# The last outputs of a two-layer decoder in single file, and weight splits behind the additions at the turn of layers

## The chip, the cores and the metric

The kernel runs on one core of one Trainium2 chip. The metric is the time of one execution on the device in microseconds (us), lower is better. TensorE (PE) multiplies into PSUM banks of 512 float32 columns; VectorE (DVE), ScalarE (ACT) and GpSimd (POOL) do the rest; SyncE (SP), ScalarE and GpSimd issue the transfers.

## What is computed

A decoder trunk of two layers on 512 tokens of width 1024, in float32, followed by a norm:

```python
def hybrid_layer(x, ...):
    z = rmsnorm(x, g_mix) @ w_in                 # q, k, v, retention q, k, v, gates
    ya = sliding_window_sink_attention(...) @ w_a
    yb = (group_norm(chunkwise_retention(...)) * silu(rg)) @ w_b
    x = x + (sigmoid(ga) * ya + sigmoid(gb) * yb) @ w_out
    h2 = rmsnorm(x, g_mlp)
    return x + jnp.square(jax.nn.relu(h2 @ w_up)) @ w_down
def reference(x, ...):
    for l in range(2):
        x = hybrid_layer(x, ...)
    return rmsnorm(x, g_final)
```

## The kernel before

**Products in three parts.** Every float32 operand is kept as a sum of two parts, hi (rounded to the matmul's own type) and lo (the rest). A product is three matmuls, hi by hi, hi by lo and lo by hi (`products`, L355 to L357). Weights come in units of 128 x 1024 elements: a DMA on SP's queue into one of five raw buffers, a ScalarE copy into hi (L308) and a VectorE subtraction into lo (L309), four buffers each. `unit` hands out the next unit and splits up to three ahead; `state["hold"]` limits how far ahead, for a while.

**Order.** The program is traced in a written order and then a scheduler with a model of times places each engine's instructions; each engine runs its own queue in the order that results. `with tc.issue_after(ins):` adds an edge that holds an instruction behind `ins` in the queue of the engine that runs `ins`, and only there; it is no wait on a semaphore.

**MLP.** The up and down projections work on blocks of 512 of the 4096 hidden units, the up projection by `pair` in halves of the tokens, the down projection by `down`, which goes through seven sums in PSUM (`multiply(a, b11)` to `multiply(b, u_forms[3])`). Results of a block are added in DRAM into `y` (tokens on partitions) by GpSimd's DMAs. The last block has another receiver, `Ending`.

**The turn of layers** (last block of layer 0). `Ending.put` adds the half i = 0 of the output columns (in `late`) on VectorE (L1352); for i = 1, `join` scales on ScalarE (L1347) and a DMA with addition (L1348) brings it to a tile `y`. `last_but_one` transposes the half i = 0 on TensorE (`turn`, L1389), adds it to x (L1395) and makes the next layer's operands xh (L378) and xl (L379) of it. The other half is turned in `carry`, within layer 1's first group, `group(..., low_last=...)`, whose first two weight units are gone through by `by_halves` (L368): all products with xh first, those with xl last. In between stand the splits of layer 1's first weights.

**The end** (last block of layer 1, `down_plain`). There are eight outputs of 128 tokens x 512 columns, each a sum over four weight units `w_end`, twelve matmuls. Three of them, `early`, go through the four units as these come; five are traced one after the other, the last in two halves of 256 columns (SOON, LATE). For each, `Ending.put` adds on VectorE (L1352), takes the squares' sum on ScalarE (L1367), and for the second half of a block's columns the root (L1375), the reciprocal (L1376) and the scaling of both halves (L1377 on VectorE, L1381 on ScalarE), and writes them out by SP (L1379) and ScalarE (L1382). For the first half it multiplies by the gain (L1369) and prepares a scalar (L1370).

Of the kernel before, what the change touches and what calls it, by code (L numbers as in the profile page):

```python
# [13 lines left out]
ALU = mybir.AluOpType  # L14
# [5 lines left out]
D = 1024  # L20
# [10 lines left out]
EPS = 1e-6  # L31
# [13 lines left out]
N_BLOCK = 8  # L45
# [69 lines left out]
def decoder(ctx, tc, xT, x_first, w_in, w_a, w_b, w_out, w_up, w_pair, w_down, w_end, tables, decay, band, g_last, out):  # L115
    nc = tc.nc
# [232 lines left out]
    def products(ps, pairs, start, stop, resume=False):  # L349


        n = len(pairs)
        for i, ((ah, al), (bh, bl)) in enumerate(pairs):
            more = {"skip_group_check": True} if resume else {}
            nc.tensor.matmul(ps, ah, bh, start=start and i == 0, stop=False, **more)  # L355
            nc.tensor.matmul(ps, ah, bl, start=False, stop=False, **more)  # L356
            nc.tensor.matmul(ps, al, bh, start=False, stop=stop and i == n - 1, **more)  # L357

    def by_halves(banks, weights, moving, ks, cols, meanwhile):

        hi, lo = weights
        for w, low in ((hi, 0), (lo, 0), (hi, 1)):
            if meanwhile and w is lo:
                meanwhile()
            for j, k in enumerate(ks):
                for c, ps in enumerate(banks):
                    first, final = k == 0 and w is hi and not low, k == KD - 1 and low
                    latest[0] = nc.tensor.matmul(ps, w[:, cols(j, c)], moving[k][low], start=first, stop=bool(final)).ins  # L368

    latest = [None]  # L370

    def split(hi, lo, src, scale=None):

# [41 lines left out]
    def group(name, layer, moving, evacuates, meanwhile=None, low_last=None):  # L415


        banks = [bank(ps_mm, "mm") for _ in range(4)]
        for u in range(4):
            if low_last:  # L420
                state["hold"] = state["next"] + 2 if u < 2 else None
            hi, lo = unit(name, layer)
            if low_last:
                by_halves(
                    banks,
                    (hi, lo),
                    moving,
                    (2 * u, 2 * u + 1),
                    lambda j, c: slice(j * T + c * P, j * T + (c + 1) * P),
                    low_last.get(u),  # L430
                )
            for j in range(0 if low_last else 2):
                k = 2 * u + j
                for c, ps in enumerate(banks):
                    cols = slice(j * T + c * P, j * T + (c + 1) * P)
                    products(ps, [((hi[:, cols], lo[:, cols]), moving[k])], k == 0, k == KD - 1)
            if meanwhile and u in meanwhile:
                meanwhile[u]()
        for ps, evacuate in zip(banks, evacuates):
            evacuate(ps)  # L440
# [17 lines left out]
    H = T // 2  # L458
# [116 lines left out]
    def layer_body(layer):  # L575
# [634 lines left out]
        def down_plain(into):  # L1210
            sums.free()

            def inner(k, m):
                if k < 2:
                    parts = [t[:, 2 * k + m // 2, (m % 2) * P : (m % 2 + 1) * P] for t in u_forms.tiles[0][0]]
                else:
                    parts = [u_two[:, r, m * P : (m + 1) * P] for r in (k - 2, k)]
                return tuple(parts)

            def add(ps, m, half, k, at=slice(0, T)):  # L1220
                cols = slice(half * T + at.start, half * T + at.stop)
                hi, lo = units[k]
                products(ps[:, : at.stop - at.start], [(inner(k, m), (hi[:, cols], lo[:, cols]))], k == 0, k == 3)

            units = []
            places = [(m, half) for m in range(NB) for half in range(2)]
            early = [(*place, bank(pool, "mm")) for place, pool in zip(places, (ps_mm, ps_aux, ps_mm))]
            for k in range(4):
                units.append(unit("w_end", layer))
                for m, half, ps in early:  # L1230
                    add(ps, m, half, k)
            for m, half, ps in early:
                into.put(half, m // 2, m % 2, ps, 1)
            for m, half in places[len(early) :]:
                final = (m, half) == places[-1]
                for at in (SOON, LATE) if final else (slice(0, T),):
                    ps = bank(ps_mm, "mm")
                    for k in range(4):
                        add(ps, m, half, k, at)
                    into.put(half, m // 2, m % 2, ps[:, : at.stop - at.start], 1, at)  # L1240

        def down(e, into):
            def multiply(ps, moving, start=True):
                hi, lo = unit("block", layer)
                for m in range(2):
                    at = slice(m * P, (m + 1) * P)
                    pairs = []
                    for k, (uh, ul) in enumerate(moving):
                        cols = slice(k * T, (k + 1) * T)
                        pairs.append(((uh[:, at], ul[:, at]), (hi[:, cols], lo[:, cols])))  # L1250
                    products(ps[m], pairs, start, True, not start)

            b11 = [(first_hi[:, k, :], first_lo[:, k, :]) for k in range(2)]
            b21, b22 = (
                [(u_two[:, k, at], u_two[:, 2 + k, at]) for k in range(2)] for at in (slice(0, H), slice(H, T))
            )
            if e == N_BLOCK - 1:
                sums.free()
            a, c = ([bank(ps_mm, "mm") for _ in range(2)] for _ in range(2))
            b = [bank(ps_aux, "b") for _ in range(2)]  # L1260
            multiply(a, b11)
            for m in range(2):
                nc.scalar.activation(b[m], a[m], AF.Copy)
            multiply(c, u_forms[0])
            for m in range(2):
                into.early(1, 1, m, c[m], -1)
            multiply(b, u_forms[1], False)
            for m in range(2):
                into.early(0, 1, m, b[m], 1)
            multiply(a, b21, False)  # L1270
            for m in range(2):
                into.put(0, 0, m, a[m], 1)
            multiply(c, b22, False)
            for m in range(2):
                into.put(0, 1, m, c[m], 1)
            if e == N_BLOCK - 1:
                state["hold"] = state["next"] + 3
            multiply(b, u_forms[2], False)
            for m in range(2):
                into.put(1, 1, m, b[m], -1)  # L1280
            into.last_but_one()
            multiply(b, u_forms[3], False)
            for m in range(2):
                into.put(1, 0, m, b[m], -1)
            into.end()
# [36 lines left out]
        class Ending:  # L1322


            def __init__(self):
                self.y, self.queued = {}, []
                for i, j in ((1, 1), (0, 1), (0, 0), (1, 0)):
                    if last:
                        two = x[:, 4 * j + 2 * i : 4 * j + 2 * i + 2, :]
                    elif i == 0:  # L1330
                        two = late_box[0][:, 2 * j : 2 * j + 2, :]
                    else:
                        two = big("y")
                    nc.gpsimd.dma_start(two, y[:, 2 * j : 2 * j + 2, i * T : (i + 1) * T])
                    for m in range(2):
                        self.y[i, j, m] = two[:, m, :]
# [17 lines left out]
            def put(self, i, j, m, ps, sign, at=slice(0, T)):  # L1354
                block = 2 * j + m
                scale = (factor if sign > 0 else negative)[:, block : block + 1]
                if i and not last:
                    self.join(i, j, m, ps, scale)
                    return
                with ExitStack() as behind:  # L1360
                    for ins in self.queued if i else ():
                        behind.enter_context(tc.issue_after(ins))
                    self.add(i, j, m, ps, scale, at)
                if last:
                    v = self.y[i, j, m]
# [1 line left out]
                    nc.scalar.activation(temp("junk")[:, at], v[:, at], AF.Square, accum_out=both if i else first)  # L1367
                    if not i:
                        nc.vector.tensor_tensor(v, v, last_gain[:, i, :], ALU.mult)  # L1369
                        self.queued.append(nc.vector.tensor_scalar(first, first, 1.0 / D, EPS, ALU.mult, ALU.add).ins)  # L1370
                        return
                    if at.stop < T:
                        nc.vector.scalar_tensor_tensor(first, both, 1.0 / D, first, ALU.mult, ALU.add)
                        return
                    nc.scalar.activation(total, both, AF.Sqrt, bias=first, scale=1.0 / D)  # L1375
                    nc.vector.reciprocal(total, total)  # L1376
                    final = nc.vector.scalar_tensor_tensor(v, v, total, last_gain[:, 1, :], ALU.mult, ALU.mult)  # L1377
                    self.queued = [final.ins]
                    nc.sync.dma_start(out[:, block, T:], v)  # L1379
                    v = self.y[0, j, m]  # L1380
                    nc.scalar.activation(v, v, AF.Copy, scale=total)  # L1381
# [2 lines left out]
            def turn(self, i, j, half, pool):  # L1384
# [7 lines left out]
                            ident,  # L1392
                        )
                xa = x[:, 4 * i + 2 * half : 4 * i + 2 * half + 2, j * H : (j + 1) * H]
                nc.vector.tensor_tensor(xa, xa, ps.rearrange("p (a t) -> p a t", t=H), ALU.add)  # L1395

            def last_but_one(self):
                if not last:
                    for half in range(2):
                        for j in range(2):  # L1400
                            self.turn(0, j, half, ps_mm)
                        for k in (2 * half, 2 * half + 1):
                            self.behind = scaled_input(k, g_mix + 2)

            def end(self):
                if not last:
# [219 lines left out]
```

## Time and profile before

| what | value |
|---|---|
| median of three runs | 1486.21 us (1484.3 to 1486.42) |
| the profiled execution's own time | 1484.08 us |
| its span, first to last instruction | 1482.3 us |
| TensorE busy | 1464.7 us |
| VectorE, ScalarE, GpSimd busy | 1079.1, 915.3, 192.6 us |
| mean granted TensorE clock | 0.997 |

A row of a timeline is: start, duration, engine, line, operation, output <- inputs, partitions x elements, count, and in brackets the engine's idle time before it with what ended it. Rows that overlap on one engine are pipelined. A row of the waits is: who waited for whom, microseconds in total, times, longest.

### The profile page before, as it was taken

The numbers are of one execution on the slowest core, as the hardware profiler recorded it, in microseconds if no ns is written. First come the engines' busy times: TensorE is split into PE (matmuls) and PEld (weight loads), VectorE is DVE, ScalarE is ACT, GpSimd is POOL, SyncE is SP. The second block draws the span as 40 slices with busy tenths as digits, with TensorE's granted clock in tenths as the row PEclk, the third lists the DMA queues.
The fourth block names the chain that finished last, engine by engine and source line by source line (L and its number), as shares of the span: only waits on it lengthen the run. The fifth ranks groups of instructions, "written<-read, shape, count | busy, mean of one in ns | idle before, by whom it ended". The sixth has DMA issues, their size and how long they took to land.

```text
span 1482.3 us, 21312 instructions
## 1 busy us (share of the span) xinstructions
PE 1464.7 (99%) x7799; PEld 1265.3 (85%) x7799; DVE 1079.1 (73%) x1639; ACT 915.3 (62%) x1501; POOL 192.6 (13%) x282
## 2 busy tenths in 40 slices
PE   9999999999999999999999999999999999999996
PEld 7888888888889999998888888888888899999995
DVE  6877668664677888888877785687447688887874
ACT  7647345532467777777765573556325777777773
POOL 0101111101001111112101012110000111111120
PEclk9999999999999999999999999999999999999998
DMA  7663996668316777776947449976443377777772
GB/s 260 186 177 98 311 265 176 178 193 215 113 51 198 192 194 190 196 183 186 304 143 211 142 131 302 250 213 161 142 128 106 105 193 188 198 192 190 194 209 90
DMA packets 92984, 272.61 MB, mean 184 GB/s; under 512 B 10832, under 2 KB 10960, under 8 KB 89040
## 3 DMA queue, kind: packets, MB, share of 16 engines
q1 hardware_dynamic: 60816, 169.27, 33.6%
q0 software_dynamic: 31344, 100.68, 31.0%
q8 instruction: 61, 1.00, 0.3%
q10 hardware_dynamic: 720, 1.31, 0.2%
q14 instruction: 43, 0.35, 0.1%
HBM read 231.37 MB, written 99.09 MB: 223 GB/s over the span
## 4 chain that ended last, share of the span: by engine, by line
PE 98%; DVE 1%; ACT 1%; DMA 0%; issue 0%; ACTq 0%
PE mm L355 25%; PE mm L357 25%; PE mm L356 25%; PE b L355 3%; PE b L356 3%; PE b L357 3%; PE rv L355 2%; PE rv L357 2%; PE rv L356 2%; PE mm L368 2%; PE score L734 1%; PE pT L699 1%; PE r L356 1%; PE r L357 1%; PE r L355 1%; PE pv L720 0%
## 5 line engine op out<-in xcount | busy, mean ns | idle before, releaser
L308 ACT ACTIVATE hi<-raw 128x1024 fp32r<-128x1024 f32 (+1 forms) x363 | 369.8, 1019 | 331.6 <-PE mm L356 224.1
L309 DVE TENSOR_TENSOR lo<-raw,hi 128x1024 fp32r<-128x1024 f32 (+1 forms) x364 | 423.7, 1170 | 168.7 <-ACT hi L308 167.5
L355 PE MATMUL mm<-xh,hi 128*128 128x512 f32 (+1 forms) x976 | 344.5, 355 | 1.1 <-ACT xh L378 0.7
L356 PE MATMUL mm<-xl,hi 128*128 128x512 f32 (+1 forms) x976 | 343.1, 354 | 0.0
L357 PE MATMUL mm<-xh,lo 128*128 128x512 f32 (+1 forms) x976 | 341.3, 355 | 0.0
L355 PE MATMUL mm<-r,hi 128*128 128x256 f32 (+1 forms) x736 | 238.6, 324 | 0.5 <-ACT mm L1181 0.5
L357 PE MATMUL mm<-r,lo 128*128 128x256 f32 (+1 forms) x736 | 238.9, 325 | 0.0
L356 PE MATMUL mm<-r,hi 128*128 128x256 f32 (+1 forms) x736 | 238.8, 324 | 0.0
L355 PEld LDWEIGHTS mm<-xh,hi 128*128 128x128 f32 x976 | 184.7, 189 | 25.8 <-ACT xh L378 1.3
L356 PEld LDWEIGHTS mm<-xl,hi 128*128 128x128 f32 x976 | 184.7, 189 | 24.2
L357 PEld LDWEIGHTS mm<-xh,lo 128*128 128x128 f32 x976 | 183.7, 189 | 24.3
L355 PEld LDWEIGHTS mm<-r,hi 128*128 128x128 f32 x736 | 139.8, 190 | 13.8 <-ACT mm L1181 0.7
L356 PEld LDWEIGHTS mm<-r,hi 128*128 128x128 f32 x736 | 139.8, 190 | 13.1
L357 PEld LDWEIGHTS mm<-r,lo 128*128 128x128 f32 x736 | 139.8, 190 | 11.3
L1320 POOL DMA_DIRECT2D y<-eu x56 | 62.2, 1353 | 370.1 <-DVE eu L1305 370.1
L356 PE MATMUL mm<-lo,r 128*128 128x512 f32 (+1 forms) x276 | 104.4, 387 | 0.0
L357 PE MATMUL mm<-hi,r 128*128 128x512 f32 (+1 forms) x276 | 101.5, 386 | 0.0
L355 PE MATMUL mm<-hi,r 128*128 128x512 f32 (+1 forms) x276 | 98.2, 389 | 0.3 <-ACT r L375 0.2
L355 PE MATMUL b<-hi,r 128*128 128x512 f32 x180 | 70.4, 391 | 0.0
L1320 POOL DMA_DIRECT2D y<-y x56 | 55.8, 1010 | 111.6 <-ACT y L1315 105.7
L356 PE MATMUL b<-lo,r 128*128 128x512 f32 x180 | 70.2, 390 | 0.0
L357 PE MATMUL b<-hi,r 128*128 128x512 f32 x180 | 67.8, 389 | 0.0
(271 smaller groups left out, 2333.1 us busy)
## 6 DMA issues: line engine op xcount, KB each, us to landing
raw<-w_in_in SPq DMA_DIRECT2D x89, 512.0 KB, 5.5
sums_down<-w_down_in POOLq DMA_DIRECT2D x30, 1024.0 KB, 11.0
sums_up<-w_pair_in POOLq DMA_DIRECT2D x56, 512.0 KB, 10.2
raw<-w_down_in SPq DMA_DIRECT2D x45, 512.0 KB, 7.5
raw<-w_pair_in SPq DMA_DIRECT2D x84, 256.0 KB, 3.7
y<-y POOLq DMA_DIRECT2D x64, 256.0 KB, 8.7
y<-eu POOLq DMA_DIRECT2D x62, 256.0 KB, 8.3
raw<-sums_down SPq DMA_DIRECT2D x30, 512.0 KB, 7.0
```

Source lines behind the costliest of these rows:

```text
L308: nc.scalar.activation(hi[:, at], raw[:, at], AF.Copy)
L309: nc.vector.tensor_tensor(lo[:, at], raw[:, at], f32(hi[:, at]), ALU.subtract)
L355: nc.tensor.matmul(ps, ah, bh, start=start and i == 0, stop=False, **more)
L356: nc.tensor.matmul(ps, ah, bl, start=False, stop=False, **more)
L357: nc.tensor.matmul(ps, al, bh, start=False, stop=stop and i == n - 1, **more)
L368: latest[0] = nc.tensor.matmul(ps, w[:, cols(j, c)], moving[k][low], start=first, stop=bool(final)).ins
L699: nc.tensor.transpose(pt[:, i * P : (i + 1) * P], sm[:, at : at + P], ident)
L734: nc.tensor.matmul(ps[:, g * w : (g + 1) * w], q_s[g][:, c, at], part[:, keys], start=i == 0, stop=i == 1)
L1320: nc.gpsimd.dma_start(y[:, 2 * j + m, i * T : (i + 1) * T], t, **how)
```

## The change

Two places change. **At the end**, `products` now records its last matmul in `latest[0]`, and each of the five outputs of `down_plain` that follow the early ones is traced under `issue_after(latest[0])`: on TensorE it stands whole behind the output before it. In `put`, an addition of the second half is queued behind the last scalar step of a first half only, no longer behind the scaling of the block before.

**At the turn of layers**, the hold on splits is set one product of `down` earlier; the split of layer 1's first unit is done by `first_weights`, on VectorE behind the two additions to x of the first half of the turned columns; the splits of the second and third unit are queued on ScalarE and VectorE behind the xh and xl of the first and of the second half (`behind`).

```diff
@@ products
-            nc.tensor.matmul(ps, al, bh, start=False, stop=stop and i == n - 1, **more)
+            latest[0] = nc.tensor.matmul(ps, al, bh, start=False, stop=stop and i == n - 1, **more).ins
+
+    latest, behind = [None], []
@@ group
         for u in range(4):
-            if low_last:
-                state["hold"] = state["next"] + 2 if u < 2 else None
-            hi, lo = unit(name, layer)
+            with ExitStack() as queue:
+                if low_last:
+                    state["hold"] = state["next"] + 2 if u < 2 else None
+                for ins in behind.pop(0) if behind else ():
+                    queue.enter_context(tc.issue_after(ins))
+                hi, lo = unit(name, layer)
@@ down_plain
                     ps = bank(ps_mm, "mm")
-                    for k in range(4):
-                        add(ps, m, half, k, at)
+                    with tc.issue_after(latest[0]):
+                        for k in range(4):
+                            add(ps, m, half, k, at)
@@ down
+            if e == N_BLOCK - 1:
+                state["hold"] = state["next"] + 3
             multiply(c, b22, False)
             for m in range(2):
                 into.put(0, 1, m, c[m], 1)
-            if e == N_BLOCK - 1:
-                state["hold"] = state["next"] + 3
             multiply(b, u_forms[2], False)
...
             multiply(b, u_forms[3], False)
+            if e == N_BLOCK - 1:
+                into.first_weights()
             for m in range(2):
                 into.put(1, 0, m, b[m], -1)
@@ Ending.put
-                with ExitStack() as behind:
-                    for ins in self.queued if i else ():
-                        behind.enter_context(tc.issue_after(ins))
+                with tc.issue_after(self.queued) if i else ExitStack():
                     self.add(i, j, m, ps, scale, at)
...
-                        self.queued.append(nc.vector.tensor_scalar(first, first, 1.0 / D, EPS, ALU.mult, ALU.add).ins)
+                        self.queued = nc.vector.tensor_scalar(first, first, 1.0 / D, EPS, ALU.mult, ALU.add).ins
...
-                    final = nc.vector.scalar_tensor_tensor(v, v, total, last_gain[:, 1, :], ALU.mult, ALU.mult)
-                    self.queued = [final.ins]
+                    nc.vector.scalar_tensor_tensor(v, v, total, last_gain[:, 1, :], ALU.mult, ALU.mult)
@@ Ending
+            def first_weights(self):
+                with tc.issue_after(self.turned):
+                    split_until(state["next"] + 1)
+
             def last_but_one(self):
                 if not last:
                     for half in range(2):
                         for j in range(2):
-                            self.turn(0, j, half, ps_mm)
+                            turned = self.turn(0, j, half, ps_mm)
                         for k in (2 * half, 2 * half + 1):
                             self.behind = scaled_input(k, g_mix + 2)
+                        if half == 0:
+                            self.turned = turned
+                            behind.append(self.behind)
+                    behind.append(self.behind)
```

`turn` now returns the instruction of its addition.

More of the change, by code (lines that the diff above doesn't have):

```diff
@@ L368, in by_halves @@
                     latest[0] = nc.tensor.matmul(ps, w[:, cols(j, c)], moving[k][low], start=first, stop=bool(final)).ins
-    latest = [None]
     def split(hi, lo, src, scale=None):
@@ L1325, in __init__ @@
             def __init__(self):
-                self.y, self.queued = {}, []
+                self.y, self.queued = {}, None
                 for i, j in ((1, 1), (0, 1), (0, 0), (1, 0)):
@@ L1394, in turn @@
                 xa = x[:, 4 * i + 2 * half : 4 * i + 2 * half + 2, j * H : (j + 1) * H]
-                nc.vector.tensor_tensor(xa, xa, ps.rearrange("p (a t) -> p a t", t=H), ALU.add)
+                return nc.vector.tensor_tensor(xa, xa, ps.rearrange("p (a t) -> p a t", t=H), ALU.add).ins
+            def first_weights(self):
+                with tc.issue_after(self.turned):
+                    split_until(state["next"] + 1)
             def last_but_one(self):
```

## The prediction

> **What bounds the kernel now.** I read the page first, then the waits of TensorE, then busy time by stretch, and last the timeline of the two places that the change touches.
>
> ```profile
> span 1482.3 us, 21312 instructions
> PE 1464.7 (99%) x7799; PEld 1265.3 (85%) x7799; DVE 1079.1 (73%) x1639; ACT 915.3 (62%) x1501; POOL 192.6 (13%) x282
> ```
>
> TensorE is busy for 1464.7 of 1482.3 us, and the change removes no product. It can only win from the 17.6 us in which TensorE is idle. Where those lie, the waits of TensorE and the stretches tell:
>
> ```profile
> PE mm L368 <- ACT xh L378: 1.7, 1, 1.7
> PE warm L335 <- DVE ones L330: 1.1, 1, 1.1
> PE mm L355 <- DVE z L853: 0.5, 1, 0.5
> ```
>
> ```profile
> 54.00:180.00 126.00, 126.00 (x613) 105.63 (x612) 92.28 (x233) 71.49 (x154) 16.43 (x30) 1.00 0.69 199
> 770.00:892.00 122.00, 121.55 (x597) 101.91 (x596) 95.32 (x243) 75.90 (x163) 12.06 (x20) 1.00 0.55 159
> 1469.60:1482.30 12.70, 0.00 (x0) 0.00 (x0) 5.68 (x14) 5.70 (x16) 0.00 (x0) 0.61 0.34 126
> ```
>
> In the second fence the columns are the stretch, its length, and the busy time of TensorE, its weight loads, VectorE, ScalarE and GpSimd. The last row is the one that matters: for 12.7 us after the last product the chip only adds, squares, scales and writes out. The wait of 1.7 us is the turn of layers (L368 is the first product of layer 1). The upper two rows are the attention of layers 0 and 1; there is next to nothing to win there.
>
> **The end: what the change does to it.** In the built program of before, TensorE's queue weaves the outputs of L1236–1239 into each other and into the three early ones; all eight finish late and in a bunch. In the changed program every output of twelve products stands whole behind the one before it. The products are the same.
>
> ```profile
> 1448.00 1.08 PE L355 MATMUL mm<-hi,r 128*128 128x512 f32 x4
> ...
> 1453.51 0.28 PE L356 MATMUL mm<-r,hi 128*128 128x256 f32 x1
> ...
> 1453.75 0.40 PE L355 MATMUL mm<-hi,r 128*128 128x512 f32 x1
> ...
> 1466.47 0.28 PE L355 MATMUL mm<-hi,r 128*128 128x256 f32 x1
> ...
> 1469.22 0.28 PE L357 MATMUL mm<-hi,r 128*128 128x256 f32 x1
> ```
>
> ```profile
> 1453.83 1.06 ACT L308 ACTIVATE hi<-raw 128x1024 fp32r<-128x1024 f32 x1 [3.53 <-PE mm L356]
> ...
> 1455.64 0.42 ACT L375 ACTIVATE r<-z 128x256 fp32r<-128x256 f32 x1
> ...
> 1476.60 0.42 ACT L1367 ACTIVATE junk<-x 128x256 f32<-128x256 f32 x1 [0.23 <-DVE sq L1373]
> ```
>
> ```profile
> 1456.10 0.42 DVE L376 TENSOR_TENSOR r<-z,r 128x256 fp32r<-128x256 f32 x1
> 1461.46 0.75 DVE L1352 SCALAR_TENSOR_TENSOR x<-mm,columns,x 128x512 f32<-128x512 f32 x1 [4.94 <-PE mm L357]
> ...
> 1467.34 0.74 DVE L1377 SCALAR_TENSOR_TENSOR x<-x,sq,late 128x512 f32<-128x512 f32 x1
> ...
> 1471.01 0.75 DVE L1377 SCALAR_TENSOR_TENSOR x<-x,sq,late 128x512 f32<-128x512 f32 x1
> ...
> 1475.35 0.87 DVE L1352 SCALAR_TENSOR_TENSOR x<-mm,columns,x 128x256 f32<-128x256 f32 x2
> 1476.40 0.16 DVE L1373 SCALAR_TENSOR_TENSOR sq<-sq 128x1 f32<-128x1 f32 x1 [0.18 <-ACT junk L1367]
> ```
>
> Between 1453.75 and 1466.47 stand 56 products, so one of 512 columns takes 0.227 us; 23 steps of 256 columns from 1466.47 to 1469.22 give 0.120. The first addition starts only at 1461.46, when TensorE is two thirds through; from there a block of 128 tokens costs VectorE and ScalarE 3.67 us (L1377 at 1467.34 and 1471.01), and the last addition runs at 1475.78, 6.3 us after its products ended at 1469.50.
>
> *The weight wait moves.* Ten products of later outputs (six of one, four of another) stood ahead of the up-projection's last twelve products (the 256-wide ones on `r`). Now they stand behind. Those twelve end 10 x 0.227 = 2.27 us sooner, the last weight split (L308, released by their L356 at 1453.79) starts at 1451.56 instead of 1453.83, and what follows it on both engines shifts by as much: L375 ends at 1453.79, L376 at 1454.25.
>
> *TensorE waits in return.* Nine products of the third weight unit run from 1453.75 - 2.27 = 1451.48 to 1453.52; the next needs L375's result, at 1453.82 with the 0.04 that such a step takes. No other product may pass, so 0.30 us are lost that before were filled with later outputs. Its rows near the end of before start in the order of the built program. The Trainium skill, "TensorE: Matmul & The Clock Gate", Part 2 (What happens when you issue a matmul), says that only weight loads are pulled ahead while matmuls keep program order, which speaks against this queue; by it the end costs those 0.30 us, without it none. The sum has the 0.30.
>
> *The drain.* Products now end at 1469.50 + 0.30 = 1469.80. Outputs finish every 12 x 0.227 = 2.72 us, two of them (5.45 us) to a block, against the 3.67 us that a block costs afterwards, so both engines are through with everything older when the last half arrives (the first three outputs end near 1455.6 now: 1453.82 + 6 x 0.227 + 0.39 of one product). Which scalar step the additions of half 1 are queued behind (`self.queued`) changes with it and costs nothing, as VectorE is waiting for TensorE here; without that cover it would be one step, 0.7 us. Step by step in the new order of VectorE: the seventh output is ready at 1466.95, its addition, the scaling of the block before and the gain product take to about 1469.1, the addition of the first half to 1469.5, then it waits. The last addition runs 1469.82 to 1470.25 (half of 0.87), L1373 behind it at 1470.27. From L1373 to the span's end there were 1482.3 - 1476.40 = 5.90 us, a chain of single steps on one half-width output that no edit touches. End: 1476.17, **6.1 us less**. Bounds: 6.4 without the 0.30; 3.8 if the weight split doesn't move and TensorE waits for L376's operand as late as before (another 2.3).
>
> **The turn of layers.**
>
> ```profile
> 729.95 0.82 PE L1389 MATMUL turn<-ident,late 128*128 128x128 f32 x6
> ...
> 734.48 2.12 PE L368 MATMUL mm<-xh,hi 128*128 128x512 f32 x8 [1.68 <-ACT xh L378]
> ...
> 741.90 1.47 PE L1389 MATMUL turn<-ident,y 128*128 128x128 f32 x12
> ```
>
> ```profile
> 728.96 1.22 DVE L309 TENSOR_TENSOR lo<-raw,hi 128x1024 fp32r<-128x1024 f32 x1
> ...
> 730.76 1.22 DVE L309 TENSOR_TENSOR lo<-raw,hi 128x1024 fp32r<-128x1024 f32 x1
> 731.89 1.91 DVE L1395 TENSOR_TENSOR x<-x,turn 128x512 f32<-128x512 f32 x3
> ```
>
> ```profile
> 732.19 0.69 ACT L1347 ACTIVATE eu<-b,columns 128x512 f32<-128x512 f32 x1 [1.19 <-PE b L357]
> 732.77 1.05 ACT L308 ACTIVATE hi<-raw 128x1024 fp32r<-128x1024 f32 x1
> 733.72 1.32 ACT L378 ACTIVATE xh<-x 128x512 fp32r<-128x512 f32 x2
> 734.95 0.62 ACT L506 ACTIVATE acc<-x 128x512 f32<-128x512 f32 x1
> ```
>
> Before, two splits on VectorE (728.96, 730.76) and one on ScalarE (732.77) stand ahead of the additions to x and the first xh. In the changed program they stand behind. All twelve transposes of `late` now go together at 729.95; from 0.82 for six and 1.47 for twelve each adds 0.11, so the ninth, the last that half 0 of x needs, ends at 731.1. VectorE takes the two additions that are ready at 730.7 and 731.3 (spacing 0.61 by the row of three); the second ends at 731.99. ScalarE starts xh at 732.01 and TensorE can go 0.76 later (733.72 to 734.48 in before): 732.77. TensorE itself is free at 734.48 - 1.68 = 732.80. The wait of 1.68 goes; nothing is left of it.
>
> *What is late next.* The second result of L1347 at this place (732.19) now stands behind two xh, one split and one square: 732.01 + 1.23 (733.72 to 734.95) + 0.95 (732.77 to 733.72) + 0.62 = 734.8. GpSimd adds it to y by DMA, and transposes in layer 1's first group need it.
>
> ```profile
> 733.24 0.85 POOL L1348 DMA_DIRECT2D y<-eu  x1 [0.94 <-ACT eu L1347]
> ```
>
> ```profile
> DMA to landing us min/median/max: 5.2/6.8/8.6
> ```
>
> ```profile
> DMA to landing us min/median/max: 8.6/8.6/8.6
> ```
>
> The first answer is for the six transfers of this line near the turn, the second for this one. Before, it landed at 733.24 + 8.6 = 741.84, and TensorE came for it at 741.90: just in time. Now it is issued 1.05 us after 734.8, at 735.85, and lands between 741.05 and 744.45. TensorE, 1.68 us ahead, does 32 products by 740.22 (7.42 us as before), then six transposes that need only older parts (0.65) and six products (1.39), and asks at 742.26. The stall is 0 to 2.2 us; I take the median row, 742.65, thus 0.4, since the loads that L309 releases (five buffers) start later and leave the transfer more room than before. The Trainium skill, "DMA: Bandwidth & Descriptors", Anatomy of one DMA, gives 2.0 us plus bytes over 436 GB/s, an estimate of 2.6 us for 256 KB: then nothing would stall and the turn would give 1.7; the rows here, 5.2 at the least, decide.
>
> *Other queues.* On SP two spills now go ahead of a weight load that waits for the moved L309; issued near 733.1 it lands 5.5 us later, and its split ran at 747.06, so 8 us cover it:
>
> ```profile
> raw<-w_in_in SPq DMA_DIRECT2D x89, 512.0 KB, 5.5
> ```
>
> ```profile
> 747.06 1.06 ACT L308 ACTIVATE hi<-raw 128x1024 fp32r<-128x1024 f32 x1 [0.80 <-PE mm L368]
> ```
>
> The moved VectorE split of the first unit (to 733.05) is needed by the ninth product, at 734.7. The hold on splits is set one product earlier (ahead of `multiply(c, b22, ...)`), which leaves the splits of the last two down units where they are in both programs and moves only the one above. The turn gives 1.68 - 0.4 = **1.3 us**, from 1.7 down to a loss of 0.5. Behind it the scheduler also orders layer 1's attention anew. Two orders of it stand in the trace, with 0.00 and 0.45 us of idle TensorE in the stretches above; I book 0, bounds -0.45 to +0.5.
>
> **Sum.** 6.1 + 1.3 = 7.4 us. The profiled execution took 1484.08 (span 1482.3 and 1.8 around it); it becomes 1476.7. It lies 2.1 under the median of the runs (1486.21, lowest 1484.3); on the median it is 1478.8. The likeliest case runs from 1475.6 (all upper bounds, 6.4 + 1.7 + 0.45 = 8.5, off the profiled execution) to 1480.5 (5.7 off the median, just short of the first rival).
>
> **Rivals.**
> *Late transfer* (14%): the moved DMA lands after 8.6 us as its like did; the turn loses 0.5, the end gives 6.1: 1480.6 by the median. For it: the DMA was just in time before. Against: fewer loads beside it.
> *Split not released* (9%): the last weight split stays where it was, TensorE stalls 2.3 us more in its fixed order: 6.1 - 2.3 + 1.3 = 5.1, 1481.1. For it: L308 waits for a buffer and for TensorE. Against: its row names TensorE's L356, which moves.
> *Bunching stays* (4%): additions and squares still go in the old pace because their own queues, not the products' order, hold them; 12.7 us of drain remain and only the turn pays: 1484.9, no change that can be measured. Against: the first addition waited 4.94 us for TensorE, by its row.
> *Attention exposed* (5%), the slower one: in the new order each of the 16 score steps of layer 1 lets TensorE wait for ScalarE's exponential.
>
> ```profile
> DVE st L758 <- ACT st L757: 4.4, 8, 1.3
> ```
>
> At the longest 1.3 us each that is 20.8 us: 1478.8 + 20.8 = 1499.6. It turns the sign beyond noise from 0.65 us a step (10.4 us). Against it: 126.00 of 126.00 us busy in layer 0's attention.
>
> **Chances.** The forecast has 68%; faster by over 0.2% (about 3 us, what a measurement here can tell from no change) takes it and the first two rivals, 0.91 together, shaded to 0.88 for what I have not seen; same 0.06, slower 0.06. The range leaves out the last two rivals: 1475.6 to 1482.
>
> **What would show it.** Right: no TensorE wait at L368 or under 0.5 us at the transposes of y; first addition of the end near 1455.6 on before's clock; about 6.4 us between last product and span's end. Wrong: a wait of TensorE for `y`; more than 1 us of wait in the last 20 us; new waits in layer 1's attention.

## The result, and the profile after

The changed kernel takes 1478.39 us (median of 8 runs, 1477.88 to 1483.20), the kernel before 1484.20 (median of 8 runs beside it, 1483.68 to 1486.45). The ratio is 0.9963, with a 95% interval of 0.9951 to 0.9974: 5.5 us faster by the means, 5.8 by the medians. One of the eight runs, at 1483.20, stands alone above the others and has no trace. Predicted were 1478.8 (1475.6 to 1482.0) and, in gain, 7.4 us. The predicted time came so near partly by luck: it was taken off a median of 1486.21, and the median of the longer series is 2.0 lower, while the gain of the medians is 1.6 smaller than the sum. The account below is of the gain.

In the changed kernel's own lines the products of the first group are L370 (L368 before), the transposes L1392 (L1389), the additions to x L1398 (L1395), the copy and the transfer into y L1353 and L1354 (L1347, L1348), the additions at the end L1358 (L1352), the last scaling L1381 (L1377), and the scaling that forms z L856 (L853).

The page and the waits of TensorE (us in all, times, longest):

```profile
span 1478.6 us, 21314 instructions
PE 1467.4 (99%) x7799; PEld 1266.5 (86%) x7799; DVE 1079.6 (73%) x1639; ACT 914.0 (62%) x1501; POOL 195.3 (13%) x282
...
PE mm L355 <- DVE z L856: 1.0, 1, 1.0
PE turn L1392 <- DMA y<-eu: 0.9, 1, 0.9
PE mm L355 <- ACT xh L378: 0.8, 1, 0.8
```

This execution took 1480.34 us, its span is 1478.6. The wait of 1.7 us at the turn is gone. Two others have grown: TensorE waits 0.9 us for the transfer into y, which stood nowhere before, and 1.0 instead of 0.5 for z. And TensorE seems to work more, 1467.4 us against 1464.7. Most of that has nothing to do with the change: 2.0 us of it are the start of this execution. The timeline of the first products, first of before, then of after:

```profile
5.45 1.17 PE L355 MATMUL mm<-xh,hi 128*128 128x512 f32 x4 [0.67 <-ACT xh L378]
6.46 1.08 PE L356 MATMUL mm<-xl,hi 128*128 128x512 f32 x4
7.38 1.08 PE L357 MATMUL mm<-xh,lo 128*128 128x512 f32 x4
```

```profile
5.64 2.08 PE L355 MATMUL mm<-xh,hi 128*128 128x512 f32 x4 [0.79 <-ACT xh L378]
7.51 1.91 PE L356 MATMUL mm<-xl,hi 128*128 128x512 f32 x4
9.22 1.41 PE L357 MATMUL mm<-xh,lo 128*128 128x512 f32 x4
```

Four products take 0.92 us from row to row in before (6.46 to 7.38), and 1.87 and 1.71 in after's first two rows. In this execution TensorE began at half its pace, and everything later stands 2.19 us later than in before, at 725.40 against 727.59 (the four transposes of `late` ahead of the turn) still. So the times of after below have to be read less 2.19. Without that start its span would be 1476.4, 5.9 under before's and close to the 5.8 between the medians.

**The turn, after.** TensorE, then the transfer:

```profile
734.98 2.11 PE L370 MATMUL mm<-xh,hi 128*128 128x512 f32 x8
...
742.37 0.81 PE L1392 MATMUL turn<-ident,y 128*128 128x128 f32 x6
742.95 1.63 PE L370 MATMUL mm<-xh,lo 128*128 128x512 f32 x6
745.46 0.87 PE L1392 MATMUL turn<-ident,y 128*128 128x128 f32 x6 [0.89 <-DMA y<-eu]
```

```profile
736.91 0.67 ACT L1353 ACTIVATE eu<-b,columns 128x512 f32<-128x512 f32 x1
...
737.94 0.85 POOL L1354 DMA_DIRECT2D y<-eu  x1 [3.62 <-ACT eu L1353]
```

```profile
DMA to landing us min/median/max: 7.5/7.5/7.5
```

Layer 1's first product starts at 732.79 on before's clock and waits for nothing (predicted 732.80). The transfer is issued at 735.75 (predicted 735.85). It lands 7.5 us later, not 6.8, and TensorE stands for 0.89. (Idle time in brackets counts from the modelled end of a product. From start to start the stop costs 1.04: the six products ahead of it take 2.51 us here, and 1.47 in join_early below, which does not stop.)

**The end, after.** The last weight split on ScalarE, TensorE around the stall and at its last product, VectorE, and the last stretch:

```profile
1453.87 1.06 ACT L308 ACTIVATE hi<-raw 128x1024 fp32r<-128x1024 f32 x1 [1.27 <-PE mm L356]
```

```profile
1455.63 0.39 PE L357 MATMUL mm<-hi,r 128*128 128x512 f32 x1
1456.16 0.97 PE L355 MATMUL mm<-hi,r 128*128 128x512 f32 x3
...
1471.96 0.28 PE L357 MATMUL mm<-hi,r 128*128 128x256 f32 x1
```

```profile
1458.08 1.41 DVE L1358 SCALAR_TENSOR_TENSOR x<-mm,columns,x 128x512 f32<-128x512 f32 x2 [1.52 <-PE mm L357]
...
1472.28 0.48 DVE L1358 SCALAR_TENSOR_TENSOR x<-mm,columns,x 128x256 f32<-128x256 f32 x1 [0.18 <-PE mm L357]
1472.68 0.15 DVE L1377 SCALAR_TENSOR_TENSOR sq<-sq 128x1 f32<-128x1 f32 x1
```

```profile
1472.24:1478.60 6.36, 0.00 (x1) 0.00 (x0) 1.47 (x4) 1.93 (x6) 0.00 (x0) 0.66 0.25 94
```

The split starts at 1451.68 on before's clock (predicted 1451.56; 1453.83 before). The first addition is at 1455.89 on before's clock (predicted near 1455.6; 1461.46 before), the last one directly behind the last product, and 6.36 us remain after it (predicted 6.35; 12.7 before). The products of the third weight unit end their steps at 1455.86 and the next starts at 1456.16: the predicted stall of 0.30.

### The profile page after: what moved, and what is told of

It reads as the page before. It is cut to its first block, busy times and chain, and to the rows that moved or that the text cites. A ratio compares the mean times of both kernels' runs of the same rounds, so it can differ in the third digit from the quotient of the medians.

```text
span 1478.6 us, 21314 instructions
## 1 busy us (share of the span) xinstructions
PE 1467.4 (99%) x7799; PEld 1266.5 (86%) x7799; DVE 1079.6 (73%) x1639; ACT 914.0 (62%) x1501; POOL 195.3 (13%) x282
## 4 chain that ended last, share of the span: by engine, by line
PE 98%; DMA 1%; ACT 1%; DVE 0%; issue 0%; ACTq 0%
PE mm L355 25%; PE mm L356 25%; PE mm L357 25%; PE b L355 3%; PE b L356 3%; PE b L357 3%; PE rv L355 2%; PE rv L357 2%; PE rv L356 2%; PE mm L370 1%; PE score L737 1%; PE pT L702 1%; PE r L356 1%; PE r L357 1%; PE r L355 1%; DMA y<-eu 1%
## 5 line engine op out<-in xcount | busy, mean ns | idle before, releaser
L355 PE MATMUL mm<-xh,hi 128*128 128x512 f32 (+1 forms) x976 | 345.2, 356 | 1.8 <-DVE z L856 1.0
L355 PE MATMUL mm<-r,hi 128*128 128x256 f32 (+1 forms) x736 | 238.8, 324 | 0.5 <-ACT mm L1184 0.5
L355 PEld LDWEIGHTS mm<-xh,hi 128*128 128x128 f32 x976 | 185.2, 190 | 26.8 <-ACT xh L378 1.5
L355 PEld LDWEIGHTS mm<-r,hi 128*128 128x128 f32 x736 | 139.8, 190 | 13.7 <-ACT mm L1184 0.7
L355 PE MATMUL mm<-hi,r 128*128 128x512 f32 (+1 forms) x276 | 98.5, 390 | 0.4 <-ACT r L375 0.2
L355 PE MATMUL b<-hi,r 128*128 128x512 f32 x180 | 70.4, 391 | 0.0
```

## The experiments

To compare kernels I read TensorE's start at four places that all have: the four transposes of `late` just ahead of the turn (725.40 in before), the first product of the chunk that follows the transposes of y (746.86), the sum of squares after the attention of layer 1 (1152.39), and the span's end (1482.3). Before's times are taken off, and the difference at the first place with them, so that the start plays no part. Negative is ahead of before, in us:

```
kernel        after the turn   after the attention   at the end
changed           -0.56              +0.15             -5.89
changed, again    -0.29              +0.45             -5.11
end_only          +0.23              +0.17             -5.49
turn_only         -0.22              +0.49             +0.88
join_early        -1.66              -1.25             -6.77
turn_late         -0.69              +0.04             -5.52
both_late         -1.61              -0.66             -6.41
late_again        -1.70              -0.77             -6.69
warm10            +1.03              +1.77             -3.80
late_warm         -1.68              -0.73             -6.69
warm_again        -1.66              -0.70             -6.57
file_oldq         -0.03              -0.02             -5.94
newq_nofile       -0.01               0.00             -1.78
```

Each is one profiled execution. Between the last two places single waits of 0.2 to 0.4 us come and go, also in kernels with the same program up to there.

**The two halves apart.** end_only keeps the edits in `down_plain` and in the ending's `put`, and undoes those in `group`, `down` and `last_but_one`; turn_only does the reverse.

> The end as changed, the turn of layers as before. Theory A, all of the gain is made at the end, and what the turn gives is taken back before the second attention is over: 1478.3 us as for the whole change (within 0.4), 5.8 less than before's usual 1484.1; the products at the turn wait 1.7 us for ScalarE's xh again, no wait for y, and the wait for z in layer 1's attention is back at 0.5. Theory B, as predicted, the turn carries 1.3 of it: 1479.6.

> The turn as changed, the end as before. Theory A: 1484.1, no change (within 0.4), although TensorE's wait for xh is gone: 0.9 us of wait for the transfer into y and 1.0 for z stand in its place. Theory B (the turn gives 1.3 as predicted): 1482.8.

end_only took 1478.59 (5 runs; ratio 0.9964, interval 0.9952 to 0.9977), turn_only 1485.24 (11 runs; 1.0003, 0.9995 to 1.0012; before beside them 1484.76). The end alone brings what the whole change brings, the turn alone nothing. The waits of TensorE in turn_only:

```profile
PE turn L1394 <- DMA y<-eu: 1.2, 1, 1.2
...
PE mm L355 <- DVE z L856: 1.0, 1, 1.0
```

Theory A holds, although turn_only missed its 1484.1 by 1.1 us: before itself stood at 1484.76 in that series. The table says where the turn's gain goes: it is 0.2 ahead after the turn instead of 1.7, and 0.5 behind after the attention.

**Is the transfer late because it is issued late?** In join_early the copy goes ahead of a weight split on ScalarE:

```
-                nc.scalar.activation(t, ps, AF.Copy, scale=scale)
+                self.joined = nc.scalar.activation(t, ps, AF.Copy, scale=scale).ins
...
                 if not last:
+                    behind[0] = (*behind[0], self.joined)
```

> The changed kernel, and ScalarE does the copy that feeds the late transfer into y ahead of one weight split (1.0 us) instead of behind it. Theory A, the transfer is late because it is issued late: issued 0.9 us sooner it lands 0.9 sooner, TensorE's wait for y falls from 0.9 to under 0.1 and TensorE is 0.9 ahead after the transposes of y; what of it is left at the end depends on the wait for z in the attention, whose order the planner writes anew (0 to 0.9; 1477.4 to 1478.3). Rival, the transfer is late because the DMA queues are full: it lands at the same moment, about 10.5 us after TensorE starts the layer's first product, the wait stays 0.9 (1478.3).

1478.98 (5 runs, 1477.10 to 1480.38; ratio 0.9961, 0.9949 to 0.9974). In the profile, of a run of 1477.10, the transfer was issued at 734.58, where turn_only had 735.47, and TensorE did not wait for it:

```profile
740.53 1.63 PE L370 MATMUL mm<-xh,lo 128*128 128x512 f32 x6
742.00 0.82 PE L1392 MATMUL turn<-ident,y 128*128 128x128 f32 x6
```

```profile
DMA to landing us min/median/max: 7.3/7.3/7.3
```

It landed at 741.88, 0.1 before TensorE came; the turn then gave its whole 1.66, and 1.25 were left after the attention. Theory A holds for this profile. The median did not move, though, and lies 0.7 above what was expected: the margin is 0.1 us, while the same transfer took between 7.3 and 9.1 us to land in the profiles of these kernels. That later landings took the gain in the other runs is the likely reason, but they have no trace.

**Asking for it later.** turn_late queues the transposes of y one pass of eight products later; both_late does this and join_early's edit:

```
-            if meanwhile and w is lo:
+            if meanwhile and low:
```

> The changed kernel, with the transposes of y in layer 1's first group queued eight products (1.8 us) later. Theory A (the wait for y is the late transfer and nothing else, and 3 us of other products stand between these transposes and the first product that needs them): TensorE's wait for y is gone in every run, also where the transfer lands 9 us after its issue; TensorE is 1.7 us ahead of before at the end of the turn and keeps 0.7 to 1.5 of it through the attention; 1477.3 (1476.8 to 1478.0) for the usual start. Rival: the additions to x and xh behind the transposes become the next late thing, a wait of TensorE for xh of up to 1.8 us stands in place of the one for y; 1478.3 or more.

> The same, and the copy that feeds the transfer ahead of one weight split, as in join_early. In this program the planner leaves the attention of layer 1 in the order that it has in the changed kernel, whose wait for z (1.0 us) stood in all profiles of that order. Theory A, each order of the attention has its own price: no wait for y, TensorE 1.7 ahead after the turn, about 1.0 of it left after the wait for z; 1477.3 (1476.9 to 1477.8). Rival, the attention takes back whatever the turn gives, because another engine is the bound there: nothing is left after the wait for z, 1478.3.

turn_late took 1479.84 (5 runs; 0.9960, 0.9948 to 0.9973), and my theory failed on it: TensorE still waited 0.8 for y (the transfer, issued at 735.87, took 7.6 us), and at 771 us it met a wait that no other kernel had:

```profile
PE mm L355 <- ACT hi L308: 1.0, 1, 1.0
PE turn L1392 <- DMA y<-eu: 0.8, 1, 0.8
```

both_late took 1477.63 (5 runs; 0.9950, 0.9937 to 0.9962). No wait for y, 1.61 ahead after the turn, but only 0.66 after the attention, where about 1.0 was expected. So 0.95 goes there, with the wait for z again 1.0:

```profile
PE mm L355 <- DVE z L856: 1.0, 1, 1.0
```

The column "after the attention" less "after the turn" sorts the kernels by the order that the planner wrote for layer 1's attention. With before's order (end_only, file_oldq, newq_nofile) it is -0.06 to +0.01. With the changed kernel's order it is 0.71 to 0.96, in eight profiles: 0.71 to 0.74 in the four that wait for y, 0.93 to 0.96 in the four that do not and come into it early; with the order of join_early 0.41 (turn_late, in that order too, has 0.73 with its own wait). It is the price of an order and not a ceiling of another engine, or both_late and join_early could have kept nothing. No run changes that order alone. VectorE shows half of it. Before, then after:

```profile
863.15 1.22 DVE L309 TENSOR_TENSOR lo<-raw,hi 128x1024 fp32r<-128x1024 f32 x1
864.29 1.28 DVE L853 TENSOR_TENSOR z<-mm,rstd 128x512 f32<-128x512 f32 x2
```

```profile
864.54 0.61 DVE L764 TENSOR_SCALAR sm<-sm,st 128x256 f32<-128x256 f32 x2
865.07 0.48 DVE L745 CUSTOM_DVE_ANT_0 sm<-score,mask,x 128x256 f32<-128x256 f32 x1
865.47 0.08 DVE L745 DVE_READ_ACCUMULATOR2_ANT st<- 128x1 f32 x1
865.47 1.22 DVE L309 TENSOR_TENSOR lo<-raw,hi 128x1024 fp32r<-128x1024 f32 x1
866.61 1.28 DVE L856 TENSOR_TENSOR z<-mm,rstd 128x512 f32<-128x512 f32 x2
```

In after a pair of softmax scalings (0.53 us of VectorE) has come between the two row maxima, ahead of the split and of z. TensorE waits for z, by 0.52 longer. The rest, 0.2 to 0.4, I could not pin to a row; nor why it is larger where TensorE comes early.

**The end taken apart.** file_oldq keeps the single file (`tc.issue_after(latest[0])`) and takes before's `self.queued` list; newq_nofile keeps the new `self.queued` and weaves the products as before. Both leave the turn as before.

> The end's single file alone (turn as before), with before's list of what an addition of half 1 is queued behind. Theory A, the order of the products makes all of the gain at the end: as end_only, 1478.5 within 0.4, last additions right behind the last products. Rival, the list holds an addition up by a step of 0.7 us or more: 1479.2 or more.

> The reverse: the changed list of what an addition is queued behind, but the products of the last outputs woven as before, turn as before. Theory A: 1484.2 within 0.5, and about 12.7 us between the last product and the end. Rival (bunching comes from the engines' own queues): 1478.5 to 1481.

file_oldq took 1478.33 (5 runs; 0.9952, 0.9939 to 0.9964): the single file alone brings the whole gain. newq_nofile took 1482.97 (11 runs; 0.9989, 0.9979 to 0.9998), and both expectations missed it: the list alone brings 1.7 us by the medians (0.3 to 3.1 by the interval), and by its profile -1.78. With the outputs in a bunch, before's list holds an addition behind the last scaling of the block before (L1377), which waits for ScalarE. Without it that addition goes first. VectorE in newq_nofile, 0.28 us later at the turn than before; in before's fence of the prediction the scaling stands at 1471.01, ahead of the addition, and the last two halves at 1475.35:

```profile
1470.09 0.74 DVE L1352 SCALAR_TENSOR_TENSOR x<-mm,columns,x 128x512 f32<-128x512 f32 x1
...
1470.94 0.75 DVE L1375 SCALAR_TENSOR_TENSOR x<-x,sq,late 128x512 f32<-128x512 f32 x1
...
1473.52 0.87 DVE L1352 SCALAR_TENSOR_TENSOR x<-mm,columns,x 128x256 f32<-128x256 f32 x2
```

In the single file VectorE waits for TensorE instead, and the list is worth nothing. The two gains do not add.

**The start.** In most series with eight dummy products the runs lie in two groups about 2 us apart (before, beside the first experiments: 10 of 15 runs from 1483.85 to 1485.05, the others from 1486.07 to 1486.76). warm10 is the changed kernel with `WARM = 10`, late_warm is both_late with it. With the latter went the changed kernel and both_late once more; warm_again repeats it.

> The changed kernel with ten instead of eight dummy products at the start. In the profile of the changed kernel the first twelve real products take 4.8 us instead of the 2.8 that they take in the profile of before, and everything after them is 2.2 us later; its runs lie in two groups about 2 us apart. Theory S1, TensorE runs at half pace because the 0.8 us without work before the first product put off its full pace: two more dummy products fill that gap, all runs fall in the lower group, 1478.2, and the first twelve products take 2.8 us. Rival S2, when the full pace begins is set by something that does not look at the gap: two groups remain, and where a run starts at half pace the first products are slow as before.

> The changed kernel once more, as the measure for the two beside it on the same chip: 1478.4 (lower group 1477.9 to 1478.6, upper group 1480.3 to 1480.9).

> both_late once more, beside the changed kernel. Theory A (the transfer on time is worth what is left of the wait for y after the attention, 0.7): 0.5 to 1.0 below the changed kernel of this call, group by group; 1477.6 and 1479.8. Rival (no more than scatter): within 0.3 of it.

> both_late with ten dummy products at the start; here no wait for y hides what the start does. Theory S1 (the gap before the first product puts off TensorE's full pace): one group of runs, 1477.4 to 1478.4, none at 1479.5 or above. Rival S2 (full pace begins by something that does not look at the gap): two groups, as in the kernels with eight, where 5 to 7 of 15 runs of before lie 2 us above the others.

> late_warm once more, since five runs could miss the upper group by chance (file_oldq, with eight dummy products, had none in five either). S1: again one group, 1477.1 to 1478.4. S2: about a third of the runs at 1479.3 or above.

warm10 took 1479.17 (5 runs, 1478.44 to 1480.89; 0.9961, 0.9948 to 0.9975) and settled nothing: its slowest run is the profiled one, whose first products ran nearly at full pace, and which lost the 2 us elsewhere:

```profile
PE turn L1392 <- DMA y<-eu: 2.5, 1, 2.5
```

```profile
DMA to landing us min/median/max: 9.1/9.1/9.1
```

In the later series the changed kernel took 1479.32 (5 runs, 1478.08 to 1480.99; 0.9963, 0.9950 to 0.9977), without the two groups that were expected, both_late 1479.50 (1477.38, 1477.47, 1479.50, 1479.53, 1480.01; 0.9958, 0.9946 to 0.9971), and late_warm 1477.68 (1477.15 to 1477.78; 0.9950, 0.9938 to 0.9963). So by the medians both_late is 0.2 behind the changed kernel, as the rival of late_again had it, by the means 0.7 ahead; in the two profiles, which both began at full pace, it is 1.6 ahead at the end. With five runs each in groups 2 us apart, the times do not show what the transfer on time is worth; the profiles do, for one execution each.

late_warm has one group, 0.6 us wide, its lowest run 0.25 under the range of S1, where both_late beside it has two. Its start:

```profile
1.07 4.64 PE L335 MATMUL warm<-ones 128*128 128x512 f32 x10 [1.07 <-DVE ones L330]
5.50 1.40 PE L355 MATMUL mm<-xh,hi 128*128 128x512 f32 x4
6.74 1.09 PE L356 MATMUL mm<-xl,hi 128*128 128x512 f32 x4
```

No idle time is left ahead of L355, and full pace comes within the first four products. warm_again took 1478.22 (5 runs, 1477.34 to 1478.61; 0.9951, 0.9937 to 0.9964), its highest 0.2 above what S1 allowed, but again with no second group. Of the 48 runs of before in these experiments 18 lie in the upper group; by S2 ten runs in a row would miss it once in a hundred times. S1 is much the likelier; a trace of each run, which would show it, there is not. Ten dummy products also do more work than eight, and no run separates that from the gap that they fill. The length of the gap alone decides nothing in a single run: in the second profile of the changed kernel TensorE stood for 1.08 us ahead of L355 and began at full pace. All runs of late_warm lie under all of the changed kernel's beside it, by 1.6 us in the median.

## Why the prediction was right, and where it was not

*The end (6.1, bounds 3.8 and 6.4).* Right, step by step: the split moved as reckoned, the stall of 0.30 came, the drain fell to 6.36. By the table's last two columns the end gave 6.04 in the profile after, and 5.5 to 6.0 in the other kernels that have it. The rivals "split not released" and "bunching stays" are out. That `self.queued` costs nothing held for the single file (file_oldq). One size beside the sum was wrong without harm: the price without that cover, put at 0.7 us, is 1.7 by newq_nofile.

*The rule of program order.* The 0.30 were booked against a trace that showed only that rows start in the program's order. The trace after has the stall, so it agrees with the Trainium skill, "TensorE: Matmul & The Clock Gate", Part 2 (What happens when you issue a matmul), that matmuls keep program order.

*The turn (1.3, from 1.7 to a loss of 0.5).* The wait of 1.68 went, as reckoned to 0.01 us. The step that failed is "what is late next": I took the median landing of six transfers, 6.8 us, and with it a stall of 0.4. The transfer itself took 7.5 us in after, 7.8 in turn_only and 9.1 in warm10, and the stalls were 0.9, 1.2 and 2.5. The second profile of the changed kernel has 7.7 and 1.2. So the landing lay between the two rows that I chose from, 6.8 and 8.6, and the stall between the 0.4 of the forecast and the 2.2 of the rival "late transfer": nearer to the forecast in the profile after, past the rival in warm10. The reason given for the lower row, that fewer loads run beside the transfer, fits in part: with the turn as before it took 8.4 to 8.9 us in four profiles, with the changed turn 7.3 to 7.8 in nine of ten. That the loads are the cause, no run shows. The way of the rival was shown: with the copy earlier and the transposes later (both_late, late_again) the turn gives 1.6 to 1.7. The estimate by the Trainium skill's "DMA: Bandwidth & Descriptors" (Anatomy of one DMA), 2.6 us, is under every landing of this line in the profile after, of which the shortest took 3.3 us:

```profile
DMA to landing us min/median/max: 3.3/4.8/7.5
```

*The attention (0, from a gain of 0.45 to a loss of 0.5).* The second term that failed: mis-sized, and outside its bounds: 0.71 lost in the profile after. I had bounded it by the waits that stood in before's two stretches; a new order made its own. The slower rival, a wait at each of the 16 score steps, did not come: one wait, for z, grew by 0.5.

Together: 6.0 for the end, 0.6 for the turn, 0.7 lost in the attention, 5.9 in the profile, where 7.4 was predicted. What the turn won did not reach the end.

## What to carry to other kernels

When every output is formed by the same number of products and a chain of work follows each, finish them one after the other, as long as a chain is shorter than the products beside it (3.67 us against 5.45 for a block here): only the last one's chain then stands behind the products. When a wait is removed, price what is queued behind the moved steps by the latest landing of that very transfer as well as by a median of its kind, and give it a margin as wide as its landings scatter (6.8 and 8.6 stood to choose from here, and 7.3 to 9.1 came). A new order from a planner has a price of its own in later stages, even if nothing there was edited; measure it by reading one engine's start at the same places of both kernels.

## What was not expected of the hardware

TensorE's first real products ran at half pace in the profile after (0.43 to 0.47 us a product instead of 0.227), after eight dummy products and 0.8 us without work, and at full pace in before after the same eight and 0.7 us. The slow start put that execution 2 us back, and the two groups of runs lie as far apart; it is the only trace of a run that began so. The Trainium skill, "TensorE: Matmul & The Clock Gate", Part 1 (What's actually happening), says that the gate watches free-running windows of activity of about 3.4 us and that the number of slow products varies from run to run. The two groups of runs agree with it, and so do the ten runs of late_warm and warm_again, where work without a gap left one group. The granted clock in the profile's rows reads 1.00 in that stretch (5.5 to 9.0) for both; the pace has to be read from the products' spacing.

One 256 KB transfer that adds into y took 7.3 to 9.1 us from issue to landing in the profiles of the same few kernels, at nearly the same place. A margin of 0.1 us in one profile says nothing about the next run.
